# First norm's modulation with four weight tiles side by side in the array's columns, 1 MB loads, and attention keys that begin with latent products

## The chip, the cores and the metric

The kernel runs on one core of one Trainium2 chip. The metric is the device time of one execution in microseconds. Before the change three executions took 1448.74, 1449.79 and 1452.77 us; the median is 1449.79 us. One more execution was recorded with the hardware profiler.

In the profile, PE is the engine of matrix products and PEld its weight loads, DVE the vector engine, ACT the scalar engine, POOL the general engine, and SP the engine whose queue issues most DMA transfers. Each works through its own instructions in order and waits on semaphores for the others.

## The reference

One layer of a diffusion backbone in float32, on 1024 latent tokens and 256 context tokens of width 1024. What the change touches is the head of it: a modulation vector from each of two conditioning vectors, the normalised inputs scaled and shifted by it, and the projection from which retention and attention take their operands.

```python
sc = jax.nn.silu(c)
scc = jax.nn.silu(c_ctx)
m_lat = sc @ w_mod[l] + b_mod[l]
m_ctx = scc @ w_mod[l] + b_mod[l]
sh1, sc1, g1, sh2, sc2, g2 = [t[:, None, :] for t in jnp.split(m_lat, N_MOD, axis=-1)]
csh1, csc1, cg1, csh2, csc2, cg2 = jnp.split(m_ctx, N_MOD, axis=-1)
h_lat = rms_norm(x, norm1_g[l]) * (1.0 + sc1) + sh1
h_ctx = rms_norm(ctx, norm1_g[l]) * (1.0 + csc1) + csh1
y_lat, y_ctx = token_mixers(h_lat, h_ctx, w_in[l], ...)
x = x + g1 * y_lat
h2 = rms_norm(x, norm2_g[l]) * (1.0 + sc2) + sh2
x = x + g2 * conv_ffn(h2, w_up[l], conv_w[l], conv_b[l], w_down[l])
return rms_norm(x, final_g)
```

`token_mixers` multiplies both inputs by `w_in` (1024 x 3584, seven blocks of 512 columns) and splits the result into retention queries, keys, values and gates and attention queries, keys and values.

## The kernel before

The width of 1024 is eight tiles of 128 rows (`KD`). Products of the large projections are made from float32 operands split in two parts, high and low, and `passes` (lines 127 to 132) issues three matrix products for each, so lines 130, 131 and 132 are seen all over the profile. The small products of the modulation are single float32 products instead.

**The first norm's modulation.** `modulation1(q)`, lines 491 to 510, is called four times. Each call makes 512 columns of shift and scale, for two tiles of the width: it loads four pieces of `w_mod` (512 KB each, two weight tiles of 128 x 512) and issues eight products into the tile `pr`. The stationary operand is `csil`, the silu of the two conditioning vectors, with two columns; the weights are the moving operand. The result has two rows. ACT copies them to `rw`, four small products with a 2 x 2 identity turn them into columns (`pm`, line 504), and DVE adds the bias and multiplies by the norm's gain into `mcol`.

**What runs beside it.** After each product `tick` (line 377) advances a generator at a set rate. Beside the first call `raw_latents` loads, normalises and transposes the first four token tiles into `xraw` (products `px`, line 558). Beside call q, `first_latents(q - 1)` scales two tiles of `xraw`, splits them into `hT` high and low, and issues 24 products `pn` of retention values for four token tiles, with one slice of block 2 of `w_in` (`more`, line 190, which calls `split_slice`: a load of 512 KB, the high part on ACT in line 183, the low part on DVE in line 184). After the last call `first_latents(3)`, then `context_rows` (the context tiles into `cT`) and `latents` (token tiles 4 to 7) run beside the products of the context and the later tokens, in `natural`. `modulate` (lines 518 to 529) transposes four tiles (line 522) into one of three buffers of PSUM, and both ACT (line 525) and DVE (line 527, `tmp`) read it before the buffer is free.

**Attention keys.** Then block 5 of `w_in` is streamed in four slices. Four products of context keys come first (`pc`, 256 columns, line 627), with `split_store`; then `modulation2(1)`, a sum over eight loads of `w_mod2` on DVE (`macc`, line 464) for the second norm; then eight products of latent keys in `transposed` (`pl`, 512 columns), which `rotated` takes through the rotary table `rtab`.

**What sets the order.** The order in the code is not the order on the engines. The framework's scheduler places the instructions of each engine by priorities and by its own estimates, and all of this is fixed when the kernel is built. Memory is handed out by pools: a pool that opens where another closed must wait until the last reader of that space has finished. Until the end of the first stage, the pool `xp` holds seven buffers of 4 KB a partition, used in turn by weight pieces and token tiles (tag `xt`). The pools `ev`, `rp` (the rotary table) and `wr` (raw weight slices, two buffers) stand beside it.

## Time and profile before

| what | us |
|---|---|
| median of three executions | 1449.79 |
| lowest, highest | 1448.74, 1452.77 |
| the profiled execution, its own time | 1450.39 |
| its span, first to last instruction | 1448.6 |
| first product of the modulation starts | 5.77 |
| PE's next work behind the last turned modulation (line 504) starts | 65.43 |
| last value product of the later tokens starts | 114.39 |
| first latent key product starts | 131.61 |

The granted clock of PE was 0.992 of full speed over the span. A row of a timeline begins with the start and the duration in microseconds and ends with the number of merged instructions; in brackets stands how long the engine was idle before it and what released it. Durations of products are modelled to their end and overlap with the next; the distance between starts is what a product costs in a row of products. A row of the table of windows gives the stretch, its length, then the busy time and instruction count of PE, PEld, DVE, ACT and POOL, the granted clock, the share of the DMA engines and GB/s. A row of the table of waits gives who waited for whom: total, number of times, longest. A row for one source line gives shortest, median and longest duration in ns.

### The profile page before, as it was taken

The numbers are of one execution on the slowest core, as the hardware profiler recorded it, in microseconds if no ns is written. First come the engines' busy times: TensorE is split into PE (matmuls) and PEld (weight loads), VectorE is DVE, ScalarE is ACT, GpSimd is POOL, SyncE is SP. The second block draws the span as 40 slices with busy tenths as digits, with TensorE's granted clock in tenths as the row PEclk, the third lists the DMA queues.
The fourth block names the chain that finished last, engine by engine and source line by source line (L and its number), as shares of the span: only waits on it lengthen the run. The fifth ranks groups of instructions, "written<-read, shape, count | busy, mean of one in ns | idle before, by whom it ended". The sixth has DMA issues, their size and how long they took to land.

```text
span 1448.6 us, 19421 instructions
## 1 busy us (share of the span) xinstructions
PE 1396.1 (96%) x6924; PEld 1142.1 (79%) x6924; DVE 1002.7 (69%) x1501; ACT 733.6 (51%) x1398; POOL 336.4 (23%) x450
## 2 busy tenths in 40 slices
PE   8999999999899989999999989999999999999996
PEld 3478778788787779999888877888888888888885
DVE  3477733443577588889455887787877877998457
ACT  3434612232355678998414754555555445455533
POOL 1230000012688522431020143222233230000001
PEclk9999999999999999999999999999999999999999
DMA  8537675465446576770422123322223324953324
GB/s 324 189 119 265 202 253 171 153 182 177 146 154 193 151 188 162 155 149 6 174 81 88 65 102 109 109 102 88 91 100 109 109 99 161 397 213 103 102 95 174
DMA packets 107529, 217.77 MB, mean 150 GB/s; under 512 B 8932, under 2 KB 47332, under 8 KB 106536
## 3 DMA queue, kind: packets, MB, share of 16 engines
q1 hardware_dynamic: 99304, 191.62, 38.6%
q0 software_dynamic: 8128, 24.91, 7.7%
q8 instruction: 55, 0.90, 0.3%
q14 instruction: 42, 0.34, 0.1%
HBM read 159.08 MB, written 57.41 MB: 149 GB/s over the span
## 4 chain that ended last, share of the span: by engine, by line
PE 71%; DVE 7%; issue 5%; DMA 4%; ACT 3%; POOL 3%; SPq 0%; POOLq 0%; DVEq 0%; ACTq 0%
PE pv L756 5%; PE chain L130 5%; PE pA L724 5%; PE chain L131 5%; PE chain L132 5%; PE c L132 4%; PE c L131 4%; PE c L130 4%; PE third L131 2%; PE third L130 2%; PE third L132 2%; PE pt L744 2%; PE pn L131 2%; PE pn L132 2%; PE pn L130 2%
## 5 line engine op out<-in xcount | busy, mean ns | idle before, releaser
L130 PE MATMUL chain<-T,whi 128*128 128x512 f32 x264 | 103.5, 393 | 6.7 <-ACT ua L1126 4.3
L130 PE MATMUL pl<-hT,whi 128*128 128x512 f32 x256 | 107.2, 419 | 0.1
L131 PE MATMUL chain<-T,whi 128*128 128x512 f32 x264 | 103.3, 391 | 0.0
L132 PE MATMUL chain<-T,wlo 128*128 128x512 f32 x264 | 103.3, 392 | 0.0
L132 PE MATMUL pl<-hT,wlo 128*128 128x512 f32 x256 | 100.6, 393 | 0.5 <-DVE wlo L184 0.5
L131 PE MATMUL pl<-hT,whi 128*128 128x512 f32 x256 | 100.7, 393 | 0.0
L727 DVE TENSOR_REDUCE mt<-pA 128x1 f32<-128x1280 f32 x64 | 95.2, 1490 | 2.8 <-PE pA L724 0.9
L724 PE MATMUL pA<-ks,qhl 128*128 128x512 f32 (+1 forms) x384 | 92.0, 376 | 4.4 <-ACT p L731 4.4
L132 PE MATMUL c<-whi,ghl 128*128 128x512 f32 x232 | 90.4, 390 | 0.0
L130 PE MATMUL c<-whi,ghl 128*128 128x512 f32 x232 | 90.3, 389 | 0.0
L131 PE MATMUL c<-wlo,ghl 128*128 128x512 f32 x232 | 90.3, 389 | 0.0
L731 ACT ACTIVATE p<-pA,mt 128x1280 f32<-128x1280 f32 x64 | 85.5, 1336 | 4.9 <-DVE mt L727 4.8
L1039 POOL TENSOR_TENSOR cmb<-wrb 128x512 f32<-128x512 f32 x20 | 28.0, 1399 | 250.3 <-DMA wrb<-w_up 179.5
L890 ACT CAST whi<-cmb 128x512 fp32r<-128x512 f32 x62 | 38.7, 624 | 88.0 <-PE chain L131 66.8
L724 PEld LDWEIGHTS pA<-ks,qhl 128*128 128x128 f32 x384 | 69.2, 193 | 17.2 <-ACT p L731 5.4
L130 PE MATMUL pn<-whi,hT 128*128 128x512 f32 x192 | 80.3, 418 | 1.9 <-ACT hT L569 1.9
L116 POOL TENSOR_TENSOR sm<-sm,mhalf 128x1 f32<-128x1 f32 x26 | 16.6, 638 | 278.9 <-DVE sm L115 278.7
L756 PE MATMUL pv<-va,aT 128*128 128x128 f32 x640 | 77.0, 276 | 0.1
L890 ACT CAST whi<-wra 128x512 fp32r<-128x512 f32 x55 | 33.8, 624 | 82.9 <-PE third L131 42.2
L131 PE MATMUL pn<-wlo,hT 128*128 128x512 f32 x192 | 75.2, 392 | 0.0
L132 PE MATMUL pn<-whi,hT 128*128 128x512 f32 x192 | 75.1, 392 | 0.0
L756 PEld LDWEIGHTS pv<-va,aT 128*128 128x128 f32 x640 | 74.0, 192 | 0.7 <-DVE yT L785 0.3
(311 smaller groups left out, 3935.1 us busy)
## 6 DMA issues: line engine op xcount, KB each, us to landing
wm<-w_mod SPq DMA_DIRECT2D x32, 512.0 KB, 4.3
raw<-w_in SPq DMA_DIRECT2D x28, 512.0 KB, 5.5
wra<-w_up SPq DMA_DIRECT2D x24, 512.0 KB, 3.4
wrb<-w_up SPq DMA_DIRECT2D x23, 512.0 KB, 3.5
W<-w_down SPq DMA_DIRECT2D x44, 256.0 KB, 6.1
ad<-s SPq DMA_DIRECT2D x20, 512.0 KB, 3.5
wra<-ad SPq DMA_DIRECT2D x20, 512.0 KB, 3.3
wrb<-ad SPq DMA_DIRECT2D x18, 512.0 KB, 3.4
```

What stands on the lines that cost most here:

```text
L116: nc.gpsimd.tensor_tensor(out=out_ap, in0=out_ap, in1=mhalf[:, :n], op=ALU.pow)
L130: mm(ps, lh, rh, start=first, stop=False, skip_group_check=more)
L131: mm(ps, lh, rl, start=False, stop=False, skip_group_check=more)
L132: mm(ps, ll, rh, start=False, stop=last, skip_group_check=more)
L724: mm(self.pa[m][:, c0:c1], self.q[:, i, m, qs], self.k[:, m, c0:c1], start=(i == 0), stop=(i == 1))
L727: nc.vector.tensor_reduce(out=self.mt[:, m : m + 1], in_=self.pa[m][:, :LK], axis=AX.X, op=ALU.min)
L731: nc.scalar.activation(self.p[m], self.pa[m][:, :LK], AF.Exp, scale=-1.0, bias=self.mt[:, m : m + 1], accum_out=self.s[:, m : m + 1])
L744: nc.tensor.transpose(self.pt[g][:, i, :], self.p[0][:, (4 * g + i) * P : (4 * g + i + 1) * P], ident)
L756: mm(self.pv, self.aT[:, c, :], self.v[:, c, :], start=(c == 0), stop=(c == NKT - 1))
L890: nc.scalar.copy(hi, src)
L1039: nc.gpsimd.tensor_tensor(out=s1, in0=b1, in1=b2, op=ALU.add)
```

## The change

**Modulation in four column groups.** The stationary operand becomes `wide`, `csil` padded with zeros to 32 columns. A call of `modulation1` loads two pieces of 1 MB with four weight tiles each, and issues the products in two groups of four. Product j of a group goes to columns 32 j to 32 j + 31 of the array (`tile_position`) and to partitions 32 j to 32 j + 31 of `pr`. The four partial sums are added when the result is turned: the 2 x 2 identity becomes `fold`, 128 rows with a one at row 32 j + s in column s. The four ticks of a group come behind its four products.

**Pools.** The weight pieces have four buffers of their own, the token tiles five. `wr` moves to the right side of the memory. The buffers of `rotated` and `split_store` move from `ev` to a new pool `er`, which, like `rp`, opens only after `xp` has closed, so the rotary table can no longer be loaded during the first stage.

**Attention keys.** Three latent products (head 0 in both halves of the tokens, head 1 in the first half) come ahead of the context keys.

```diff
-XT = 7
...
+        late = p1.enter_context(ExitStack())
+        wr = late.enter_context(tc.tile_pool(name="wr", bufs=2, side="right"))
...
-        rp = p1.enter_context(tc.tile_pool(name="rp", bufs=1))
-        late = p1.enter_context(ExitStack())
-        wr = late.enter_context(tc.tile_pool(name="wr", bufs=2))
...
-            hl = ev.tile([P, 2, 512], F32R, name="xhl")
+            hl = er.tile([P, 2, 512], F32R, name="xhl")
...
-            xa = ev.tile([P, 512], F32, name="xa")
-            xb = ev.tile([P, 512], F32, name="xb")
+            xa = er.tile([P, 512], F32, name="xa")
+            xb = er.tile([P, 512], F32, name="xb")
...
-            bsc = xp.tile([P, KD], F32, name="bsc", bufs=1)
+            bsc = xp.tile([P, 64], F32, name="bsc")[:, :KD]
+            wide = xp.tile([P, KD, 32], F32, name="wide")
+            nc.vector.memset(wide, 0.0)
+            nc.vector.tensor_copy(wide[:, :, 0:2], csil)
+            fold = xp.tile([P, 64], F32, name="fold")[:, :2]
+            nc.vector.tensor_copy(fold, ident[:, 0:2])
+            for j in range(1, 4):
+                nc.vector.tensor_tensor(out=fold, in0=fold, in1=ident[:, 32 * j : 32 * j + 2], op=ALU.add)
...
-                for kk in range(KD // 2):
-                    raw = xp.tile([P, 2, 512], F32, name="wt", tag="xt", bufs=XT)
-                    nc.sync.dma_start(out=raw, in_=w_mod[q][:, 2 * kk : 2 * kk + 2, :])
-                    for j in range(2):
-                        mm(pr[:2, :], csil[:, 2 * kk + j, :], raw[:, j, :], start=(kk + j == 0), stop=(kk + j == KD // 2))
+                for kk in range(2):
+                    raw = xp.tile([P, 4, 512], F32, name="wt", bufs=4)
+                    nc.sync.dma_start(out=raw, in_=w_mod[q][:, 4 * kk : 4 * kk + 4, :])
+                    for j in range(4):
+                        mm(pr[32 * j : 32 * j + 32, :], wide[:, 4 * kk + j, :], raw[:, j, :], start=(kk == 0), stop=(kk == 1), tile_position=(0, 32 * j), skip_group_check=True)
+                    for j in range(4):
                         tick()
-                rw = xp.tile([2, 512], F32, name="rw", bufs=2)
-                nc.scalar.copy(rw, pr[:2, :])
+                rw = xp.tile([P, 512], F32, name="rw", bufs=1)
+                nc.scalar.copy(rw, pr)
...
-                    mm(pm[:, j, :], rw[:, j * P : (j + 1) * P], ident[:2, :2], start=True, stop=True)
+                    mm(pm[:, j, :], rw[:, j * P : (j + 1) * P], fold, start=True, stop=True)
...
-                    xt = xp.tile([P, D], F32, name="xt", tag="xt", bufs=XT)
+                    xt = xp.tile([P, D], F32, name="xt", bufs=5)
...
+        er = p1.enter_context(tc.tile_pool(name="er", bufs=2))
+        rp = p1.enter_context(tc.tile_pool(name="rp", bufs=1))
...
+        transposed(wg, dk_d, rtab, 32, 1.0, LC, by_head[:3])
         for h in range(H):
...
-        transposed(wg, dk_d, rtab, 32, 1.0, LC, by_head)
+        transposed(wg, dk_d, rtab, 32, 1.0, LC, by_head[3:])
```

The order on three engines moves at the places below. A row is the line of the kernel's file, the operation, the tile written and the tiles read, and the shape; `x3` stands for equal rows in succession. Line numbers of the changed file differ.

PE from the second turned modulation on, before: `pr` is the modulation, `pn` the value products of the first tokens.

```order
L504 MATMUL pm<-ident,rw 128x2 x4
L498 MATMUL pr<-wt,csil 2x512 x3
L130 MATMUL pn<-whi,hT_168 128x512
L131 MATMUL pn<-wlo,hT_168 128x512
L132 MATMUL pn<-whi,hT_170 128x512
L498 MATMUL pr<-wt,csil 2x512
L130 MATMUL pn<-whi,hT_168 128x512
L131 MATMUL pn<-wlo,hT_168 128x512
L132 MATMUL pn<-whi,hT_170 128x512
```

PE at the same place in the changed kernel.

```order
L510 MATMUL pm<-fold,rw 128x2 x4
L503 MATMUL pr<-wt,wide 32x512 x4
L129 MATMUL pn<-whi,hT_171 128x512
L130 MATMUL pn<-wlo,hT_171 128x512
L129 MATMUL pn<-whi,hT_171 128x512
L130 MATMUL pn<-wlo,hT_171 128x512
L131 MATMUL pn<-whi,hT_173 128x512
L129 MATMUL pn<-whi,hT_171 128x512
L130 MATMUL pn<-wlo,hT_171 128x512
L131 MATMUL pn<-whi,hT_173 128x512 x2
L503 MATMUL pr<-wt,wide 32x512 x4
```

Between two turned modulations there were one group of three products and five single ones, each between value products; now there are two groups of four, with nine value products between them and fifteen behind the second.

DVE around the last modulation, before: lines 115 and 516 normalise token tiles (`xt`), 508 and 510 make `mcol`, 184 splits a weight slice, 568 scales the first tokens, 571 makes the low part, 527 begins with the context.

```order
L516 TENSOR_SCALAR xt<-xt,sm 128x1024
L115 TENSOR_SCALAR sm<-sm 128x1
L516 TENSOR_SCALAR xt<-xt,sm 128x1024
L508 TENSOR_TENSOR mcol<-pm,bsc 128x2x2
L508 TENSOR_TENSOR mcol<-pm,cl 128x2x2
L510 TENSOR_TENSOR mcol<-mcol,cl 128x2x2
L184 TENSOR_TENSOR wlo<-raw,whi 128x1024
L568 TENSOR_SCALAR xraw<-xraw,mcol 128x512 x2
L571 TENSOR_TENSOR hT_170<-xraw,hT_168 128x512
L527 TENSOR_SCALAR tmp<-pt,mcol 128x256 x2
```

DVE at the same place in the changed kernel (lines 114 and 522 normalise, 514 and 516 make `mcol`, 574 scales, 577 makes the low part, 533 begins with the context).

```order
L514 TENSOR_TENSOR mcol<-pm,bsc 128x2x2
L514 TENSOR_TENSOR mcol<-pm,cl 128x2x2
L516 TENSOR_TENSOR mcol<-mcol,cl 128x2x2
L574 TENSOR_SCALAR xraw<-xraw,mcol 128x512 x2
L114 TENSOR_SCALAR sm<-sm 128x1
L522 TENSOR_SCALAR xc_504<-xc_504,sm 128x1024
L577 TENSOR_TENSOR hT_173<-xraw,hT_171 128x512
L114 TENSOR_SCALAR sm<-sm 128x1
L522 TENSOR_SCALAR xt<-xt,sm 128x1024
L533 TENSOR_SCALAR tmp<-pt,mcol 128x256 x2
```

The split of the first slice of block 5 and three of the four normalisations of token tiles 4 to 7 stood ahead of the context work; the split and those three now stand behind it, one normalisation and one context tile between.

SP while block 5 is loaded, before: `wm` are the loads for `modulation2`, `raw` the weight slices, `kvg` stores of values; the row of `raw` is the last slice of block 5.

```order
L463 DMA wm_1086<-w_mod 128x1024
L405 DMA kvg_82<-st 128x512
L463 DMA wm_1089<-w_mod 128x1024
L641 DMA mk<-consts 128x256
L642 DMA kd<-consts 128x8
L463 DMA wm_1092<-w_mod 128x1024
L405 DMA kvg_83<-st 128x512
L180 DMA raw<-w_in 128x1024
L463 DMA wm_1095<-w_mod 128x1024
```

SP in the changed kernel, from the rotary table to that slice.

```order
L214 DMA rtab<-rope 128x2048
L403 DMA kvg_79<-st 128x512
L403 DMA kvg_82<-st 128x512
L458 DMA macc<-rows 1x1024
L461 DMA wm_1183<-w_mod 128x1024
L403 DMA kvg_82<-st 128x512
L461 DMA wm_1186<-w_mod 128x1024
L646 DMA lp<-rows 128x256
L647 DMA lg<-rows 128x8
L461 DMA wm_1189<-w_mod 128x1024
L650 DMA dec<-consts 128x1024
L461 DMA wm_1192<-w_mod 128x1024
```

The last slice of block 5 was issued behind seven loads of `wm`; now it stands two rows below the last one shown, behind four, and the rotary table, which was loaded ahead of block 5, is loaded behind its first three slices and ahead of all `wm`.

More of the change, by code (lines that the diff above doesn't have):

```diff
@@ L548, in raw_latents @@
                 for t in range(4):
-                    xt = xp.tile([P, D], F32, name="xt", tag="xt", bufs=XT)
+                    xt = xp.tile([P, D], F32, name="xt", bufs=5)
                     nc.sync.dma_start(out=xt, in_=x[t * P : (t + 1) * P, :])
```

## The prediction

> **What bounds the kernel now.** I read the page's busy shares first, then the table of windows over the first 130 us, then the timeline of PE from one modulation to the next.
>
> ```profile
> span 1448.6 us, 19421 instructions
> PE 1396.1 (96%) x6924; PEld 1142.1 (79%) x6924; DVE 1002.7 (69%) x1501; ACT 733.6 (51%) x1398; POOL 336.4 (23%) x450
> ...
> 10.00:20.00 10.00, 10.00 (x46) 4.04 (x44) 6.22 (x11) 6.06 (x10) 1.66 (x3) 1.00 1.02 413
> 30.00:40.00 10.00, 10.00 (x33) 3.88 (x32) 3.53 (x7) 2.67 (x4) 1.29 (x1) 1.00 0.50 157
> ```
>
> PE is busy for 96% of the span, so a microsecond taken from PE's own queue, anywhere, should arrive at the end. The front is where the change works. From 10 to 20 us the DMA engines run full (413 GB/s, about 0.41 MB per us, so 1.28 us for 512 KB); from 30 to 40 us they are half idle and PE is full. So after some 25 us the front waits for PE, not for the weights. One modulation to the next looks like this on PE:
>
> ```profile
> 20.23 1.05 PE L504 MATMUL pm<-ident,rw 2*128 2x2 f32 x8
> ...
> 34.20 1.05 PE L504 MATMUL pm<-ident,rw 2*128 2x2 f32 x8
> 35.18 2.74 PE L498 MATMUL pr<-wt,csil 128*2 128x512 f32 x6
> 37.84 0.50 PE L130 MATMUL pn<-whi,hT 128*128 128x512 f32 x1
> 38.18 0.39 PE L131 MATMUL pn<-wlo,hT 128*128 128x512 f32 x1
> 38.41 0.40 PE L132 MATMUL pn<-whi,hT 128*128 128x512 f32 x1
> 38.73 1.02 PE L498 MATMUL pr<-wt,csil 128*2 128x512 f32 x2
> 39.69 0.50 PE L130 MATMUL pn<-whi,hT 128*128 128x512 f32 x1
> ...
> 49.32 1.05 PE L504 MATMUL pm<-ident,rw 2*128 2x2 f32 x8
> ...
> 64.45 1.05 PE L504 MATMUL pm<-ident,rw 2*128 2x2 f32 x8
> 65.43 0.89 PE L522 MATMUL pt<-ident,xc 128*128 128x128 f32 x6
> ```
>
> A period from pm to pm is 15.12 us (34.20 to 49.32). The trace has two records for each f32 product pr, 64 records for 32 products, and they follow each other at 0.43 us:
>
> ```profile
> L498 PE MATMUL pr<-wt,csil x64: 591/592/1061, 5.8 to 62.3; 128*2 128x512 f32 x64
> ...
> 21.20 0.09 PEld L498 LDWEIGHTS pr<-wt,csil 128*2 128x2 f32 x2
> 21.63 0.08 PEld L498 LDWEIGHTS pr<-wt,csil 128*2 128x2 f32 x1 [0.34 <-issue]
> ...
> 109.63 0.39 PE L132 MATMUL pn<-whi,hT 128*128 128x512 f32 x1
> ...
> 114.39 0.39 PE L132 MATMUL pn<-whi,hT 128*128 128x512 f32 x1
> ```
>
> So eight products are 16 x 0.427 = 6.83 us. The 24 products pn go at 0.227 us each (21 starts from 109.63 to 114.39), 5.45 us. Going from pr to pn and back costs about 0.3 us: 38.73 to 39.69 is 0.96 instead of 0.85, and 37.84 to 38.73 is 0.89 instead of 0.68. Six such breaks are 1.8. pm is 0.98. The sum, 15.06, is the period measured: there is no wait in it, and only PE work can shorten it.
>
> **The products in the array's columns.** In the changed kernel the eight products of a modulation stand in two groups of four, each of the four on its own 32 columns. Let S be the time of such a group. A period is then 2 S + 5.45 + 2 breaks (0.6) + 0.98 = 2 S + 7.03. No row shows two products side by side, so S has bounds. It can't be under the two records of one product, 0.86; one behind the other it is eight records, 3.42. I take 2.14. The records of one product use the same columns, so the second must wait for the first, and the rows show records starting in program order, with one set of weights loaded ahead (two loads at 21.20, then one each 0.43). If that order holds across columns, product 1's first record can start beside product 0's second, but not before it: eight records fall into five slots of 0.43. The row nearest to this is the 0.43 step itself.
>
> The Trainium skill, "TensorE: Matmul & The Clock Gate", Part 3 (packing small matmuls), says that products on different columns run at once, starts some 4 ns apart, three of 32 columns 2.38 times as fast, and also that matmuls start and end strictly in program order. The first taken alone puts S near 0.86 (a rival below), the second with two records to a product gives my five slots; no row here can choose.
>
> **The start.** The first loads change:
>
> ```profile
> 6.94 1.06 ACT L514 ACTIVATE sq<-xt 128x1024 bf16<-128x1024 f32 x1 [3.76 <-DMA xt<-x]
> 9.76 1.09 PE L558 MATMUL px<-ident,xt 128*128 128x128 f32 x8 [0.63 <-DVE xt L516]
> 11.32 1.06 ACT L514 ACTIVATE sq<-xt 128x1024 bf16<-128x1024 f32 x1 [0.29 <-DMA xt<-x]
> 19.43 0.57 ACT L501 COPY rw<-pr 2x512 f32<-2x512 f32 x1
> ```
>
> The third tile of x landed at 11.3 us as the fifth half megabyte (two loads of w_mod, three of x), and still does (one load of 1 MB, three of x). The second 1 MB load lands at 11.3 + 2 x 1.28 = 13.9, the fourth x at 15.2. From an x tile landing to its transposes takes 2.82 us (6.94 to 9.76), so px of the third ends at 11.32 + 2.82 + 1.09 = 15.2, and group two follows: 15.2 + S. ACT then copies rw (0.57) ahead of the fourth tile's square, and 2.82 + 1.09 + 0.98 later pm ends: 20.7 + S, against 21.2 now. The copy of 128 partitions instead of two has the same 512 columns, so I keep 0.57. The memset, copies and three additions for wide and fold stand on DVE while it waits for the first x; pm has the same count and moving columns. All these I cost at nothing; uncovered, they would be under 1 us together by DVE's rows of this size.
>
> Three periods follow. With S = 2.14: 20.7 + 2.14 + 3 x 11.31 = 56.8, against 65.43 now: **8.6 us gained**. The next hT is hidden under group one:
>
> ```profile
> 35.28 0.16 DVE L508 TENSOR_TENSOR mcol<-pm,bsc 128x4 f32<-128x4 f32 x1 [9.33 <-PE pm L504]
> 36.26 1.14 ACT L569 CAST hT<-xraw 128x512 fp32r<-128x512 f32 x2 [2.96 <-DVE xraw L568]
> ```
>
> The first of the two casts ends at 36.83, 1.65 after pm; a group shorter than that would wait. Loads don't bind: a period takes 2.5 MB, 6.4 us at the full rate.
>
> **After the last modulation.**
>
> ```profile
> 56.23 0.76 DVE L516 TENSOR_SCALAR xt<-xt,sm 128x1024 f32<-128x1024 f32 x1 [0.67 <-POOL sm L116]
> ...
> 65.81 1.23 DVE L184 TENSOR_TENSOR wlo<-raw,whi 128x1024 fp32r<-128x1024 f32 x1
> ...
> 68.20 0.50 PE L130 MATMUL pn<-whi,hT 128*128 128x512 f32 x1 [1.88 <-ACT hT L569]
> ...
> 70.00:80.00 10.00, 9.65 (x50) 7.23 (x50) 8.65 (x20) 6.71 (x14) 3.39 (x4) 1.00 0.15 56
> 80.00:90.00 10.00, 8.35 (x48) 6.31 (x47) 8.21 (x15) 5.09 (x7) 5.07 (x3) 1.00 0.14 52
> ...
> PE pt L522 <- DVE tmp L527: 1.9, 3, 0.8
> ```
>
> DVE split a weight slice (1.23 us at 65.81) ahead of the scaling that PE waited 1.88 us for; in the changed order that split comes later, and the wait falls to about 1.2 (the 1.65 us of hT less 0.45 of transposes): 0.7 gained. But DVE, busy 8.65 and 8.21 of 10 us here, gets work that it did before while it idled: three of the four normalisations (0.75 each) and that slice, 3.5 us. PE, in order behind the transposes of these tiles, already waits 1.9 us for DVE here. Bounds: nothing, or all 3.5. I take another 1.9, net **1.2 lost** (from 0.7 gained to 2.8 lost).
>
> **Attention keys.**
>
> ```profile
> PE pc L132 <- DVE wlo L184: 1.7, 2, 1.5
> PE pc L130 <- ACT whi L183: 0.9, 1, 0.9
> ...
> 117.24 0.33 SPq L180 DMA_DIRECT2D raw<-w_in x1
> ...
> 121.39 1.05 ACT L183 CAST whi<-raw 128x1024 fp32r<-128x1024 f32 x1 [5.93 <-DMA raw<-w_in]
> ```
>
> The context products (256 columns) run through the four weight slices of block 5 faster than these come: PE waits 2.6 us, last for a slice whose load was issued at 117.24, behind seven loads of the second norm's modulation. With latent products first, six k-steps are 18 x 0.227 = 4.1 us instead of about half of that, the order puts the other half's first products behind them, and the late slice is loaded behind four such loads. I take **2.4 gained** of 2.6. Bounds: all 2.6; or 1.5 lost, if the macc operations that stand ahead of the splits on DVE wait for their own loads, which now queue behind the rope table (1 MB). The table itself must wait for xp's space; the 16 us of latent value products hide that, and its first use comes after a whole product. Context keys cost the same later. From block 6 on the orders agree but for single rows; I count nothing there, give or take 1 us.
>
> **Sum.** 8.6 - 1.2 + 2.4 = 9.8 us. The profiled execution took 1450.39 us (1.8 outside its span), so 1440.6; the median, 1449.79, lies 0.6 lower: **1440 us**.
>
> **Rivals.** *All four at once*: if the array starts product 1 while product 0's second record still waits, S = 0.86. Group one then hides under the 1.65 us of hT, a period is 1.65 + 0.86 + 7.03 = 9.54, and the modulations end at 20.7 + 0.86 + 28.6 = 50.2, 15.2 gained: 1433.4. For it: the columns share nothing. Against: the records start in order. This is the skill's packing table taken for each record.
>
> *No overlap*, the change not doing what it says: S = 3.42, period 13.87, end 20.7 + 3.42 + 41.6 = 65.7; only the net 1.2 of the later parts less 0.3 is left: 1448.9. For it: every two records in this trace follow each other.
>
> *Slower*: if tiles in columns lose the load ahead, each record pays its load and its full length, 0.083 + 0.592, so S = 5.4, period 17.8, end 79.6, 14.2 lost: 1463. With 7 S on the path it is slower by more than 0.3% from S = 4.2. Against: two weight loads stand at one time in the row above. The Trainium skill, "TensorEngine Tiling (Array Packing)", Key Properties, says that changing the tiling mode drains the array, and this kernel changes it 16 times; nothing here shows its price, and my breaks of 0.3 us already hold the trace's own changes of form.
>
> **Chances.** Five slots 0.50, at 1437 to 1446 with the bounds of the later terms; four at once 0.25, at 1431 to 1439; no overlap 0.17; slower 0.08. The range, 1431 to 1446, leaves out most of the last two. 0.3% is 4.3 us, about what a measurement of this kernel can tell from no change. Faster by more: 0.25 and nearly all of 0.50, 0.72; within: 0.20; slower: 0.08.
>
> **What would show it.** Right: pm to pm near 11.3 us; pr records of different columns that start together in pairs, a group over in 2.1 us; the last pm ending near 57; under 0.5 us of PE waiting for block 5; DVE as releaser of two to four microseconds of PE's waits between the last pm and the value products. Wrong: pm to pm of 9.5 or 14; a wait for wt or raw in the periods; a PE wait for tmp or xt far above 4 us, which would say that DVE, not PE, sets the stage after the modulations; or the front's gain given back before block 6.

## The result, and the profile after

| | before | after |
|---|---|---|
| median of four executions each, same chip, us | 1450.66 | 1436.66 |
| lowest and highest, us | 1448.74 to 1452.77 | 1435.59 to 1438.61 |
| ratio, with its 95% interval | | 0.9905 (0.9886 to 0.9923) |
| span of the profiled execution, us | 1448.6 | 1434.9 |

The change makes the kernel faster by 14 us, 1%. The forecast was 1440, in a range of 1431 to 1446. The page of the changed kernel begins:

```profile
span 1434.9 us, 19409 instructions
PE 1374.9 (96%) x6924; PEld 1143.0 (80%) x6924; DVE 1005.9 (70%) x1507; ACT 732.6 (51%) x1398; POOL 336.6 (23%) x450
```

PE is as full as before, with the same 6924 instructions, and the span is 13.7 us shorter: the time came out of PE's own queue. The timeline of PE in the changed kernel, from the second turned modulation to the last (start, duration, engine, line):

```profile
34.02 0.95 PE L510 MATMUL pm<-fold,rw 128*128 128x2 f32 x8
34.89 1.06 PE L503 MATMUL pr<-wt,wide 128*32 128x512 f32 x8
36.65 0.50 PE L129 MATMUL pn<-whi,hT 128*128 128x512 f32 x1 [0.69 <-ACT hT L575]
...
39.20 1.06 PE L503 MATMUL pr<-wt,wide 128*32 128x512 f32 x8
40.20 0.50 PE L129 MATMUL pn<-whi,hT 128*128 128x512 f32 x1
...
43.75 0.95 PE L510 MATMUL pm<-fold,rw 128*128 128x2 f32 x8
...
53.48 0.95 PE L510 MATMUL pm<-fold,rw 128*128 128x2 f32 x8
54.45 0.69 PE L528 MATMUL pt<-ident,xc 128*128 128x128 f32 x3
```

A period is 9.73 us (43.75 to 53.48) where it was 15.12 and the forecast said 11.3. A group of four products is over in 1.00 us (39.20 to 40.20), with the change of form behind it, and not in 2.14. The table of windows of the changed kernel, for the tile `pr` alone, in slices of 0.05 us, shows why (stretch, length, busy time of PE, PEld and ACT with the records touched, granted clock, DMA share, GB/s):

```profile
39.20:39.25 0.05, 0.05 (x4) 0.05 (x8) 0.00 (x0) 1.00 1.02 410
...
39.65:39.70 0.05, 0.05 (x8) 0.00 (x0) 0.00 (x0) 1.00 0.87 328
```

Four records run from the first slice on, with all eight weight loads beside them; at 39.65 the first four end and the other four begin. So a group is two steps of 0.43 us, not five.

Where the 13.7 us arise, place by place on PE (start of the instruction named):

| place | before | after | gained so far |
|---|---|---|---|
| first turned modulation | 20.23 | 22.34 | -2.1 |
| last turned modulation | 64.45 | 53.48 | 11.0 |
| last value product of the later tokens | 114.39 | 104.88 | 9.5 |
| first gate of `modulation2` (block 5 is over) | 187.79 | 175.99 | 11.8 |
| second gate of `modulation2` | 261.13 | 248.88 | 12.25 |
| next work, `pk` | 264.49 | 250.70 | 13.8 |
| end of the span | 1448.6 | 1434.9 | 13.7 |

The front could have given more than 11 us. PE runs at half pace at first, waits, and then runs at half clock once more. PE in the changed kernel, and the window around it (here busy time of PE, PEld, DVE, ACT and POOL ahead of the clock):

```profile
7.27 1.93 PE L503 MATMUL pr<-wt,wide 128*32 128x512 f32 x8 [7.27 <-DMA wt<-w_mod]
11.22 3.67 PE L564 MATMUL px<-ident,xt 128*128 128x128 f32 x16 [2.01 <-DVE sm L114]
...
16.75 1.06 PE L503 MATMUL pr<-wt,wide 128*32 128x512 f32 x8
21.26 1.28 PE L564 MATMUL px<-ident,xt 128*128 128x128 f32 x8 [3.45 <-DVE xt L522]
22.34 1.71 PE L510 MATMUL pm<-fold,rw 128*128 128x2 f32 x8
23.97 1.93 PE L503 MATMUL pr<-wt,wide 128*32 128x512 f32 x8
...
20.00:30.00 10.00, 8.74 (x41) 5.73 (x41) 4.64 (x9) 2.17 (x4) 1.60 (x2) 0.66 1.01 401
```

The first group takes 1.93 us and the second 1.06: the program begins at half pace. The table's clock reads 1.00 there, but this trace holds no record of the clock before 15.1 us, so the durations have to tell. PE stands still for 3.45 us before the fourth token tile's transposes; from some 22 us on the granted clock is half. A mean of 0.66 over 10 us is 6.8 us of half clock, and the products show it: a group takes 1.93 again. So the first period is 11.68 us (22.34 to 34.02), about 2 longer than the others. Why the transposes came late stands on ACT:

```profile
8.40 1.06 ACT L520 ACTIVATE sq<-xt 128x1024 bf16<-128x1024 f32 x1 [5.28 <-DMA xt<-x]
...
12.37 0.59 ACT L567 COPY xraw<-px 128x512 f32<-128x512 f32 x1 [1.50 <-PE px L564]
12.85 1.06 ACT L520 ACTIVATE sq<-xt 128x1024 bf16<-128x1024 f32 x1
17.88 0.59 ACT L507 COPY rw<-pr 128x512 f32<-128x512 f32 x1 [0.88 <-PE pr L503]
18.36 1.06 ACT L520 ACTIVATE sq<-xt 128x1024 bf16<-128x1024 f32 x1
```

The first tile of x, behind 1 MB of weights in place of 512 KB, lands 1.46 us later (its square starts at 8.40, before at 6.94). The copy of its transposes stands on ACT ahead of the third tile's square, which so begins at 12.85 and not at 11.32. The modulation's second group follows the third tile's transposes at 16.75, and the fourth tile's square stands behind the copy of the group's result. One microsecond and a half is handed from queue to queue; by the copy, which came 1.15 us behind the first transposes here and 0.69 before, some 0.5 of it is the half pace, an estimate.

And at the second gate the kernel before had half clock where the changed kernel has not. First the row of before, then that of after:

```profile
261.13 3.57 PE L469 MATMUL pg<-macc,ones 128*128 128x512 f32 x4 [2.75 <-DVE macc L464]
```

```profile
248.88 1.98 PE L467 MATMUL pg<-macc,ones 128*128 128x512 f32 x4 [2.30 <-DVE macc L462]
```

The same four products cost 3.57 and 1.98 us, and 1.6 us of the gain is this. PE waited 2.75 us ahead of them before and 2.30 after. Over all fourteen profiles of this study, the four with the longer products, 2.76 to 3.61, have waits of 2.31 to 3.43 there; the ten with 1.98 have waits of 1.19 to 2.39. So by and large the half clock goes with the length of the wait, which is 1.41 in a second profile of the change. Whether the change shortened it, one profile of the kernel before can't tell.

### The profile page after: what moved, and what is told of

Same layout as the page of the kernel before. It is cut to its first block, busy times and chain, and to the rows that moved or that the text cites. A ratio compares the mean times of both kernels' runs of the same rounds, so it can differ in the third digit from the quotient of the medians.

```text
span 1434.9 us, 19409 instructions
## 1 busy us (share of the span) xinstructions
PE 1374.9 (96%) x6924; PEld 1143.0 (80%) x6924; DVE 1005.9 (70%) x1507; ACT 732.6 (51%) x1398; POOL 336.6 (23%) x450
## 4 chain that ended last, share of the span: by engine, by line
PE 66%; DVE 7%; issue 5%; DMA 5%; POOL 3%; ACT 3%; POOLq 0%; SPq 0%; DVEq 0%; ACTq 0%
PE pv L765 5%; PE chain L129 5%; PE chain L131 5%; PE chain L130 5%; PE pA L733 5%; PE c L131 4%; PE c L130 4%; PE c L129 4%; PE third L129 2%; PE third L131 2%; PE third L130 2%; PE pt L753 2%; PE pn L130 2%; PE pn L131 2%; PE pn L129 2%
## 5 line engine op out<-in xcount | busy, mean ns | idle before, releaser
L900 DVE TENSOR_TENSOR wlo<-cmb,whi 128x512 fp32r<-128x512 f32 x62 | 58.7, 951 | 22.9 <-ACT whi L899 22.9
```

The lines of the kernel that those rows point to most:

```text
L900: nc.vector.tensor_tensor(out=lo, in0=src, in1=r32(hi), op=ALU.subtract)
```

## The experiments

Medians are compared with runs of the kernel before on the same chip; places are read from each run's profile.

**Same columns.** All of the change but the columns: `csil` is the stationary operand again, and the products follow each other.

```diff
-  mm(pr[32 * j : 32 * j + 32, :], wide[:, 4 * kk + j, :], raw[:, j, :], start=(kk == 0), stop=(kk == 1), tile_position=(0, 32 * j), skip_group_check=True)
+  mm(pr[:2, :], csil[:, 4 * kk + j, :], raw[:, j, :], start=(kk + j == 0), stop=(kk + j == 4))
...
-  mm(pm[:, j, :], rw[:, j * P : (j + 1) * P], fold, start=True, stop=True)
+  mm(pm[:, j, :], rw[:, j * P : (j + 1) * P], ident[:2, :2], start=True, stop=True)
```

> The changed kernel with the eight products of a modulation on the same two columns again, in two groups of four, loads, pools and key order as changed. Theory one (the gain of the front is the four column groups running at once, so that a group takes 0.9 to 1.0 us instead of 3.42): a group here takes 3.4 us, pm to pm is 2 x 3.42 + 7.0 = 13.9 us against 9.7 in the changed kernel, and the span is 3 x 4.1 = 12 us plus about 2 us of the start longer than the changed kernel's 1434.9, so 1447 to 1450, the old time. Rival (the gain is the large loads, or the four ticks together that keep the value products in one stretch): pm to pm stays under 11 us and the span under 1440.

Measured: 1451.06 us (1447.04 to 1453.52) against 1450.84, ratio 0.9995 (0.9982 to 1.0007). PE of this run:

```profile
34.80 1.05 PE L510 MATMUL pm<-ident,rw 2*128 2x2 f32 x8
35.77 3.60 PE L503 MATMUL pr<-wt,csil 128*2 128x512 f32 x8
...
48.72 1.05 PE L510 MATMUL pm<-ident,rw 2*128 2x2 f32 x8
...
63.95 1.05 PE L510 MATMUL pm<-ident,rw 2*128 2x2 f32 x8
```

A group takes 3.6 us again and the last turned modulation is back at 63.95. The whole measurable gain needs the columns; without them, loads of 1 MB, pools and the order of the keys move the median by nothing that can be measured. From the last modulation to the last value product it is 48.93 us here (63.95 to 112.88), 49.94 in the kernel before and 51.40 in the changed one; this is used below.

**Context keys first.** Only the order of the attention keys is undone.

```diff
-        transposed(wg, dk_d, rtab, 32, 1.0, LC, by_head[:3])
...
-        transposed(wg, dk_d, rtab, 32, 1.0, LC, by_head[3:])
+        transposed(wg, dk_d, rtab, 32, 1.0, LC, by_head)
```

> The changed kernel with the context keys ahead of all latent keys, as before the change; the modulation as changed. Theory one (the late weight slice of the key block is what the latent products cover): PE waits 2 to 2.7 us again for splits of that block, the changed kernel's 0.88 us wait is gone, and the first product of the second norm's modulation for the gate comes 1.5 to 2.5 us later relative to the last value product than in the changed kernel, span 1436 to 1437.5. Rival (the new pools alone did it, or the order costs as much as it saves): waits and span as in the changed kernel, 1434 to 1435.5.

Measured: 1442.77 us (1442.21 to 1443.44), ratio 0.9942 (0.9925 to 0.996). From the last value product to the first gate it takes 73.94 us (106.84 to 180.78), the changed kernel 71.11, both at a granted clock of 1.00: the order of the keys is worth 2.8 us there. PE waits 1.2 us for the split of a slice of block 5 and 1.3 us ahead of the small products of `modulation2`, which theory one didn't have; the changed kernel waits 0.9 us for a split of block 5 and not there. It isn't worth that in the run with the same columns, which has the new order and takes 73.38, as the kernel before (73.40): PE waits 2.5 us there for splits of block 5 (1.8 for the high part, 0.7 for the low). Why these come late behind a slow front was not tested. The span, 1440.4, is 2.9 above theory one's upper bound. Most of that is the start, which is not part of the edit (PE's order is the same up to 105 us), and yet differs:

```profile
15.75 1.94 PE L564 MATMUL px<-ident,xt 128*128 128x128 f32 x8 [0.86 <-DVE xt L522]
17.62 1.93 PE L503 MATMUL pr<-wt,wide 128*32 128x512 f32 x8
23.00 1.94 PE L564 MATMUL px<-ident,xt 128*128 128x128 f32 x8 [3.45 <-DVE xt L522]
24.73 1.71 PE L510 MATMUL pm<-fold,rw 128*128 128x2 f32 x8
```

The same wait of 3.45 us, but products took twice their time already ahead of it (1.94 for the eight transposes that the change's profile has at 1.07, in both at 15.75). Here the half pace of the start lasts on: the trace's first record of the clock, with full clock, stands at 30.6 us, in the change's at 15.1. The modulation is 2.4 us later than there (22.34), without a change in the program.

**Tokens first.** The four row loads of x go ahead of the first weight loads.

```diff
-                    nc.sync.dma_start(out=xt, in_=x[t * P : (t + 1) * P, :])
-                    yield
+                    nc.sync.dma_start(out=xt, in_=x[t * P : (t + 1) * P, :])
+                    xts.append(xt)
+                yield
+                for t, xt in enumerate(xts):
...
             beside(raw_latents(), 1.5, 1.0)
+            next(side["g"])
             modulation1(0)
```

> The changed kernel with the loads of the first four token tiles ahead of all of w_mod; all else as changed. Theory one (the changed kernel loses 2 us at the start against the old one, because the fourth token tile lands behind 2 MB of w_mod and its square waits on ACT behind the copy that waits for the second group; PE then idles over 3 us and runs at half clock from 22 to 28.8 us): the first pm starts at 14 to 16 us instead of 22.3, no half clock before 30 us, the last pm starts 7 to 10 us earlier than 53.5 unless the weights become the limit (12 MB at 0.41 MB per us, 33 us), span 1426 to 1429. Rival (the loads are the limit from then on, or a later stage gives it back): last pm not before 50, span 1432 to 1435.

Measured: 1434.95 us (1433.26 to 1439.75), ratio 0.9895 (0.9876 to 0.9913). The first turned modulation starts at 18.49, 3.9 us earlier, but the last at 50.65, only 2.8 earlier. The first period is 12.4 us: PE waits 1.76 us for the first `hT` behind the modulation, and half clock follows (the mean from 20 to 24 us is 0.70). So the order of the loads is worth less than was expected.

**Clock kept.** Four products (eight records) that nothing reads fill PE's wait at the start of the change.

```diff
+                    if t == 3:
+                        for i in range(4):
+                            mm(part[0], ones, prev[:, 0:512], start=True, stop=True)
+                    prev = xt
```

> The changed kernel with four float32 products of 512 columns that nothing reads (0.85 us each at full clock), put on PE where it waits for the fourth token tile. Theory one (the first period of 11.7 us instead of 9.7 is the half clock that PE got after those waits): the first pm starts at 21.5 to 23 us as now, the clock stays full from 16 to 40 us, pm to pm is 9.7 us in the first period too, and the last pm starts about 2 us earlier, at 51.5. Rival (the first period is long for a load or a split that comes late): the first period stays 11 us or more at full clock.

Measured: 1435.37 us (1433.13 to 1438.15), ratio 0.9891 (0.9871 to 0.991). PE of this run:

```profile
18.48 2.84 PE L560 MATMUL pn<-xt,ones 128*128 128x512 f32 x6
...
22.04 0.95 PE L510 MATMUL pm<-fold,rw 128*128 128x2 f32 x8
...
31.84 0.95 PE L510 MATMUL pm<-fold,rw 128*128 128x2 f32 x8
...
51.32 0.95 PE L510 MATMUL pm<-fold,rw 128*128 128x2 f32 x8
...
50.00:60.00 10.00, 7.91 (x41) 5.78 (x40) 7.08 (x15) 5.98 (x13) 3.94 (x5) 1.00 0.01 4
```

With no wait from 16 to 22 us there is no half clock: the first period is 9.80, and the last modulation starts 2.16 us earlier than in the change. So the half clock behind the wait costs 2 us. All profiles of this study with the wait of 3.45 us, five of them, have products at half pace right behind it (in the run with the context keys first they were so ahead of it too); the three in which it is filled in this way have none there. The last row is used below. In the medians 2 us of 1436 can hardly be told from nothing.

**Tokens first and clock kept.** Both, with the unread products behind the first modulation, where tokens first had its wait.

```diff
             modulation1(0)
+            for i in range(4):
+                mm(part[0], ones, xraw[:, 7, :], start=True, stop=True)
```

> Edit: the four row loads of x ahead of the first weight loads, as in the run before with tokens first, and four float32 products of 128x512 that nothing reads behind the first modulation's folding products, where TensorE stood idle for 1.8 us and half clock followed. Output as the reference's. Theory one (the new start is held up by order and by the clock, and the two add): the idle 19.5 to 21.3 us is gone, no granted clock under 1.00 between 20 and 30 us, the last modulation's folding products start 1 to 2 us earlier than the 50.65 us of the run with tokens first, and the time is 1432.5 to 1434.5. Rival (from the second modulation on the transfers set the pace, at a DMA share of 1.0 until 28 us): the clock is kept and the last folding products still start at 50 to 51 us; the time stays at 1434.5 to 1436.

Measured: 1435.02 us (1433.59 to 1441.49), ratio 0.989 (0.987 to 0.991). The clock is 1.00 from 20 to 30 us, and the last modulation starts at 51.10, 0.1 us past the rival's bound, with a time within it: the two don't add. Of the time between, 20 to 28 us shows a DMA share of 1.02. That the transfers set this pace was not tested by itself. None of the three versions is told apart from the change by its median.

**Columns in turn.** Both pieces of 1 MB are loaded first, and the products stand in the order of columns 0, 0, 1, 1, 2, 2, 3, 3.

```diff
-                    for j in range(4):
-                        mm(pr[32 * j : 32 * j + 32, :], wide[:, 4 * kk + j, :], raw[:, j, :], ...)
+                    raws.append(raw)
+                for j in range(4):
+                    for kk in range(2):
+                        mm(pr[32 * j : 32 * j + 32, :], wide[:, 4 * kk + j, :], raws[kk][:, j, :], ...)
```

> Edit: both 1 MB pieces of a group are loaded first, and the eight products go in the order column 0, 0, 1, 1, 2, 2, 3, 3 in place of 0, 1, 2, 3, 0, 1, 2, 3. Output as the reference's. Theory one (each group of columns takes its own records as they come and none waits for another column's): the eight products, sixteen records, four in each column, end within 4 x 0.43 = 1.7 to 2.0 us of the first, and the time is within 3 us of the change's 1436.7. Rival (a record that waits for its own column holds back those of the other columns that stand behind it): thirteen slots of 0.43 us, 5.5 us for the eight products in place of 2.1, and 8 to 12 us more in all, 1445 to 1449.

Measured: 1440.6 us (1436.95 to 1444.12), ratio 0.993 (0.9907 to 0.9953). One product of each modulation went alone, early; the other seven stand on PE in the order of columns 0, 1, 1, 2, 2, 3, 3 and are fourteen records, two of column 0 and four of each other. PE and PEld of this run:

```profile
40.78 1.94 PE L506 MATMUL pr<-wt,wide 128*32 128x512 f32 x14
42.65 0.73 PE L131 MATMUL pn<-whi,hT 128*128 128x512 f32 x2
...
40.78 0.17 PEld L506 LDWEIGHTS pr<-wt,wide 128*32 128x32 f32 x8 [0.36 <-issue]
41.24 0.14 PEld L506 LDWEIGHTS pr<-wt,wide 128*32 128x32 f32 x3 [0.29 <-issue]
41.67 0.14 PEld L506 LDWEIGHTS pr<-wt,wide 128*32 128x32 f32 x3 [0.29 <-issue]
```

Fourteen records in 1.87 us, four steps of 0.43 with the change of form. The weight loads come as eight at once, then three, then three: one for each column that is at work and one ahead for it, until column 0 has nothing left. So records of column 3 start while those of column 1, which stand ahead of them, still wait: each group of columns takes its own, and none holds up another. By the rival's rule these seven products would have taken eleven slots, 4.7 us. The time is 2.7 us above that of the change on the same chip (1437.86, below); in the profile, where seven of the eight products of a modulation stand behind the second piece, the last modulation starts at 56.97.

**Two columns.** Columns 0, 1, 0, 1 in a group of four.

```diff
-  mm(pr[32 * j : 32 * j + 32, :], ..., start=(kk == 0), stop=(kk == 1), tile_position=(0, 32 * j), ...)
+  mm(pr[32 * (j % 2) : 32 * (j % 2) + 32, :], ..., start=(kk == 0 and j < 2), stop=(kk == 1 and j > 1), tile_position=(0, 32 * (j % 2)), ...)
```

> Edit: two groups of columns in place of four; in a piece the four products go to columns 0, 1, 0, 1, and the folding adds two rows in place of four. Output as the reference's. Theory one (records of different columns run at once, those of one column one after the other): a group of four products takes 4 x 0.43 = 1.7 to 1.9 us in place of 1.0, and the time lies between that of four columns (1436.7) and of one (1451.1), at 1440.5 to 1443. Rival (what was written ahead of the change: two records of one product in one column hold back the next column): five slots of 0.43, 2.1 us or more in a group, 1443 to 1446.

Measured: 1440.17 us (1436.82 to 1445.26), ratio 0.9925 (0.9904 to 0.9945); the median is just under theory one's 1440.5. PE of this run:

```profile
42.92 1.05 PE L510 MATMUL pm<-fold,rw 64*128 64x2 f32 x8
43.90 1.91 PE L503 MATMUL pr<-wt,wide 128*32 128x512 f32 x8
...
53.92 1.05 PE L510 MATMUL pm<-fold,rw 64*128 64x2 f32 x8
```

A group takes 1.91, four steps of 0.43 and its end. With one, two and four columns a group takes 3.60, 1.91 and 1.06 us, and a period at full clock 13.92, 11.00 and 9.73. The period falls by less than the two groups do in both steps, by 2.9 for 3.4 and by 1.3 for 1.7. With four columns the next `hT` is no longer covered (PE waits 0.69 for it at 36.65 above); with two, the nine value products behind the first group take 2.70 us (45.74 to 48.44), with one 2.26.

**The change again.** No edit, on the chip of the last three.

> Edit: none, the change once more, beside the three others on one chip. Theory one (where the half clock falls at the start varies from execution to execution, without any change in the program): first folding products at 22 to 25 us, last at 53 to 56, time 1435 to 1439. Rival (the clock follows the program): the same windows of half clock as in the profile of the change, 22 to 28.8 and 56 to 59.5 us, and the last folding products at 53.5 within 0.2.

Measured: 1437.86 us (1434.57 to 1441.69), ratio 0.9904 (0.9886 to 0.9923). The profiled execution is as the rival said, with 22.31 and 53.58 for the first and last turned modulation. It doesn't settle the question, since the run with the context keys first has another start with the same program up to there. Later on this profile does differ from the first: it has a mean clock of 0.98 between the last value product and the first gate, where that had 1.00, and 73.06 us in place of 71.11 for it. PE waits longer for one split of a weight slice, 2.52 us in place of 1.29, and half clock follows:

```profile
169.81 0.79 PE L129 MATMUL pn<-whi,cT 128*128 128x512 f32 x1 [2.52 <-ACT whi L184]
```

So two executions of one program differ by 2 us in this stretch alone, and a difference between two profiles, such as the 2.8 us of the keys, is to be read with care. The six profiles with the new order, a fast front and a clock of 1.00 there take 70.15 to 71.26 us, which speaks for the 2.8.

**Scaling on ACT.** The stretch behind the last modulation is 51.40 us in the change and 48.93 with the same columns. Two theories: half clock, which the change has at 56 us, or DVE, which gets work there that it did before while it idled. Clock kept answers the first already: its clock from 50 to 60 us is 1.00 (its last row above), and its stretch is 51.37. For the second, the scaling of the context and of token tiles 4 to 7 goes to ACT, on top of clock kept, and on the change alone.

```diff
-                nc.vector.tensor_scalar(out=xt, in0=xt, scalar1=sm[:, col : col + 1], scalar2=None, op0=ALU.mult)
+                if col in range(2, 6):
+                    nc.vector.tensor_scalar(out=xt, in0=xt, scalar1=sm[:, col : col + 1], scalar2=None, op0=ALU.mult)
+                else:
+                    nc.scalar.activation(xt, xt, AF.Identity, scale=sm[:, col : col + 1])
```

> Edit: on top of the run in which four unread products keep the clock, the scaling of the two context tiles and of token tiles 4 to 7 by the reciprocal root goes from DVE to ACT: six instructions of 0.75 us off DVE, on ACT some 1.06 us each (by its square of the same tile). Output as the reference's. From the last modulation's folding products to the last value product it was 51.4 us in that run and 48.9 us with all products in the same columns, both at full clock. Theory one (what makes these 2.4 us is DVE, which gets the scaling as work of that stretch, since the faster modulation leaves no idle time for it before): the stretch falls to 49 to 50 us, PE's waits in it from 4.1 to under 3 us, and the time to 1433 to 1434.5. Rival (the stretch is bound by the latency of the chain of transposes, ACT and DVE, whichever does the scaling, or ACT becomes late instead): 51 us or more, and 1435 or more.

> Edit: the same six scalings on ACT, on the change as it is (no unread products). Output as the reference's. Theory one (DVE makes the stretch behind the last modulation long, not the half clock there): from the folding products to the last value product 49 to 50.5 us in place of 51.4, with or without half clock at 56 us; time 1434.5 to 1436.5. Rival (the half clock at 56 us is what it costs): 51 us where the clock is at half, and the time stays at 1436.5 to 1438.

Measured: 1435.89 us (1433.76 to 1440.14), ratio 0.9912 (0.9894 to 0.993), and alone 1440.2 (1438.59 to 1442.77), ratio 0.9937 (0.9922 to 0.9951). The stretches are 51.47 (53.16 to 104.63) and 51.75. Theory one fell. In the first 30 us of the stretch DVE is busy for 21.39 us in place of the 25.08 of clock kept, and ACT for 25.03 in place of 18.35, and PE now waits for ACT too, 0.84 us for one tile. So this doesn't clear DVE: ACT may have become late in its place, as the rival says. Alone the ratio is 0.9937 where the change has 0.9905, and the time lies beyond both theories; its profile has the half pace of the start up to 19.9 us, the last modulation at 55.26, and half clock once more before the first gate. The window and a row of PE from the first of the two runs:

```profile
53.16:83.16 30.00, 26.82 (x137) 19.82 (x135) 21.39 (x47) 25.03 (x40) 12.94 (x12) 1.00 0.19 62
...
72.58 0.55 PE L531 MATMUL pt<-ident,xt 128*128 128x128 f32 x3 [0.84 <-ACT xt L525]
```

**Normalisation early.** If not the amount of work, then its place: the loads and the normalisation of token tiles 4 to 7 are written into the fourth modulation, ahead of the context, on top of clock kept and on the change alone.

```diff
                     nc.sync.dma_start(out=raw, in_=w_mod[q][:, 4 * kk : 4 * kk + 4, :])
+                    if q == 3 and kk == 1:
+                        for _ in range(4):
+                            next(later)
...
-            beside(latents(), 0.75, 3.0)
+            beside(later, 0.75, 3.0)
```

> Edit: on top of the run in which four unread products keep the clock, the loads and the whole normalisation of token tiles 4 to 7 are written into the fourth modulation, behind its second load, in place of behind the context tiles. Output as the reference's. In that run three of the four normalisations stood behind the context's work on ACT and DVE (scaled together 19 us after the last folding products), and the stretch from those products to the last value product took 51.4 us; moving the scaling alone to ACT left it at 51.5. Theory one (the order is what makes the stretch long: the transposes of tiles 4 to 7 wait for normalisations that stand late in the queues): those transposes begin 16 us behind the folding products in place of 20 to 21, the stretch falls to 49 to 50 us and the time to 1433 to 1434.5. Rival (the stretch is bound by the sum of DVE's or ACT's work in it, or the context tiles, whose loads now queue behind 2 MB, become late): 51 us or more and 1435 or more.

> Edit: the same on the change as it is, without the unread products; a version that could be used. Output as the reference's. Theory one: stretch 49 to 50 us in place of 51.4, time 1434.5 to 1436, wherever the half clock at the start falls. Rival: 51 us or more, 1436.5 to 1438.

Measured: 1447.41 us (1444.63 to 1449.31), ratio 0.9975 (0.9964 to 0.9986), and alone 1449.43 (1445.71 to 1454.31), ratio 0.9992 (0.9979 to 1.0005). A miss, and a dear one. The stretch is 54.43 us on top of clock kept (51.52 to 105.95) and 54.82 alone. ACT, PE and SP of that run:

```profile
54.01 1.05 ACT L523 ACTIVATE sq<-xt 128x1024 bf16<-128x1024 f32 x1
...
55.56 1.04 ACT L184 CAST whi<-raw 128x1024 fp32r<-128x1024 f32 x1
...
56.66 1.22 PE L129 MATMUL pn<-whi,hT 128*128 128x512 f32 x2 [4.19 <-ACT whi L184]
...
41.24 22.58 SPq L181 DMA_DIRECT2D raw<-w_in x3
...
114.23 0.80 PE L129 MATMUL pl<-hT,whi 128*128 128x512 f32 x1 [3.15 <-ACT whi L184]
```

The squares, early now, push the split of the last weight slice of block 2 back on ACT (44.59 in clock kept, 55.56 here), and PE waits 4.19 us for it, with half clock behind (0.50 from 56 to 60 us). Until that slice is split its buffer isn't free, and SP stands at the next load of `raw`: three loads take 22.58 us of its queue. PE waits for a slice again in block 5, 3.15 us at 114.23. The transposes of tiles 4 to 7 began 18.6 us behind the last modulation, for all four tiles; in clock kept the first of the four began at 13.4 and the other three at 20.2. That is less than was expected, and it bought nothing: what the early squares hold up is worth more. Whether another order would give the 2.4 us back stays open.

## Why the forecast was right, and where it was not

| step | forecast, us | in the profiles, us |
|---|---|---|
| front, up to the last modulation | 8.6 gained | 11.0 gained |
| behind it, up to the last value product | 1.2 lost | 1.5 lost |
| attention keys | 2.4 gained | 2.3 gained |
| all later parts | 0, give or take 1 | 1.9 gained |
| sum | 9.8 | 13.7 |

**What bounds the kernel** was read rightly: the front waited for PE's queue, and what was taken from it arrived at the end.

**The columns.** The step that failed is "if that order holds across columns". From the rows of one column (one record each 0.43 us, one set of weights ahead) it took a rule for all, and so got five slots. The group's windows show two steps of four, and columns in turn shows lines of their own for each group of columns. So the mechanism that held was the first rival's, four at once, with S near 1.0, the step to the value products included, where it had 0.86, and its period of 9.54 was measured as 9.73. It had been given a chance of 0.25, the five slots 0.50. The Trainium skill, "TensorE: Matmul & The Clock Gate", Part 3 (packing small matmuls), gives both rules: products on different columns run at once, and the trace agrees (four records in the first 0.05 us); starts in strict program order, and the measurement differs, at least for records that stand behind one that waits for its own column.

**Why then not the rival's 1433.4.** It had the modulations end at 50.2; PE's next work starts at 54.45. Of the 4.25 us between, 2.4 are in the first modulation (PE's next work after it starts at 23.97, forecast 20.7 + 0.86 = 21.6), where the step "group two follows at 15.2" missed the copy on ACT ahead of the third tile's square; group two started at 16.75, and some 0.65 is half clock in the folding products (1.63 for 0.98). Another 1.4 are the first period; by clock kept, whose first period is 9.79 so counted, 1.1 of them are half clock, which no term held, and 2 us in all go with it. The other 0.45 is in the two periods that follow, 9.73 each for 9.54. The forecast of 1440 lies within 3.4 us of the median because these two omissions stand against a gain per group that was put too low; in that the number was lucky. The 11 us are themselves those of one profile of each kernel: with the half pace of the start up to 30.6 us the last modulation starts at 55.63, which is 8.8 us gained.

**After the last modulation.** The net was close, and the two parts have the right sign: with the same columns the new order alone saves 1.0 us of the stretch (49.94 to 48.93; forecast 0.7), and the fast front costs 2.5 again (51.40; forecast 1.9). The reason given, DVE's extra work, isn't shown: the two waits of before, 1.9 and 1.9 us, fell to 1.5 and 1.0, only 0.6 is new, and scaling on ACT took work off DVE and left the stretch as long, though with PE waiting for ACT. PE's waits of the stretch in the changed kernel (who waits for whom, total, times, longest):

```profile
PE pt L528 <- DVE tmp L533: 1.5, 3, 0.8
PE pn L129 <- ACT hT L575: 1.0, 1, 1.0
PE pn L131 <- POOL hT L535: 0.3, 2, 0.2
PE pn L131 <- DVE hT L535: 0.3, 1, 0.3
```

Nor is it the half clock there: at 0.57 from 56 to 60 us it takes 1.7 us of PE's pace, and the stretch is as long as with full clock, so other waits cover it. What is left is the order of the scaled tiles, transposes and splits among ACT, DVE and PE; that is an argument, and no run shows it.

**Keys.** 2.3 us in the profiles and 2.8 by the run that undoes them, at the forecast of 2.4. The wait itself gave less: the 2.6 us for splits of block 5 fell by 1.7, since PE still waits for one split, where under 0.5 was expected:

```profile
PE pl L129 <- ACT whi L184: 0.9, 1, 0.9
```

That the order is worth nothing while the front is slow was not foreseen.

**Later parts.** Of the 1.9 us, 1.6 are the half clock at the second gate, in the one profile of the kernel before and in neither of the two of the change; no term of the forecast held it. Whether it is an effect of the change or luck stays open. Without it the gain by the medians, 14.0 us, would still be 12.4.

**No overlap** and **slower** are out: without overlap the time is 1451, and no drain is seen. A step from `pr` back to `pn` (39.20 to 40.20) costs 0.15 us over two steps of 0.427; the Trainium skill, "TensorEngine Tiling (Array Packing)", Key Properties, speaks of a drain at a change of mode, and if there is one, it is no longer than that here.

## What to carry to other kernels

When small products use a few columns of the array, put different ones on different groups of columns and count the records of each group by itself: the longest group sets the time, and the order of the program among groups matters little. Then look at what the freed time uncovers: here the waits of the first tokens, a few microseconds of standstill with half clock behind them, and a stretch behind them that became 2.5 us longer for a reason that wasn't found. Moving work earlier in one queue is not free either; see first which split, copy or load stands behind it.

## What the runs showed of the hardware

- Four records of different columns run together at 0.43 us each, as one alone does; the weights of eight load within 0.17 us. One, two and four groups of columns: 3.60, 1.91, 1.06 us for eight records.
- The start runs at half pace (1.93 for 1.06 us of a group of four columns, 5.94 for 3.60 of one). In three profiles of the same instructions it ends by 15.1, 15.7 and 30.6 us, where the trace's first record of the clock stands, and the first turned modulation starts at 22.34, 22.31 and 24.73. Ahead of the first record the table reads 1.00: the durations tell the pace there, not the record.
- A wait of 3.45 us on PE near the start was followed by 6.8 us of half clock (0.66 of full over 10 us), a wait of 1.76 us by some 3.4; with products in the long wait there was none. Later, waits of 2.52 us (block 6, in one of two executions; 1.29 in the other) and of 2.75 to 3.43 us (second gate) had half clock behind them. At the second gate 2.31 us had it in part and 2.39 in another run not, so these profiles give no sharp bound.
- Half clock need not cost anything: in the stretch after the modulations 3.4 us of it (0.57 of full over 4 us) left the stretch at 51.40, against 51.37 at full clock.
